# A side chain that waits for its conditioning, weight loads moved from ACT to SP, split sums in the norms, and unused products in a two-block kernel

## The chip, the cores and the metric

The kernel runs on one core of one Trainium2 chip. The metric is the device time of one execution in microseconds (us). Five engines work in parallel, each through its own instructions in the order in which they were written: PE (TensorE, matrix products; its weight loads are listed as PEld), DVE (VectorE), ACT (ScalarE), POOL (GpSimd) and SP (SyncE, which here only issues DMAs). An instruction that waits holds up all that stands behind it on its engine.

## The reference, cut to what matters

Two transformer blocks over 512 tokens of width 1024, all in float32. The first (`first_block`) has a gating unit, a sparse attention, an attention over a memory of 256 tokens, and a feed-forward part. The second (`second_block`) has two layers, and carries a context of 256 tokens beside the 512:

```python
for l in range(DEPTH_2):
    m = (jax.nn.silu(c) @ w_mod[l] + b_mod[l]).reshape(B, N_MOD, D_MODEL)          # conditioning
    mc = (jax.nn.silu(c_ctx) @ w_mod[l] + b_mod[l]).reshape(1, N_MOD, D_MODEL)
    x = ffn_sublayer(x, m, 0, norm_g[l, 0], ffn_w_in[l, 0], ffn_w_out[l, 0])
    xc = ffn_sublayer(xc, mc, 0, norm_g[l, 0], ffn_w_in[l, 0], ffn_w_out[l, 0])   # context
    h, hc = mod_norm(x, m, 1, norm_g[l, 1]), mod_norm(xc, mc, 1, norm_g[l, 1])
    ...                                                 # mixers, attention over h and hc
    x = ffn_sublayer(x, m, 2, norm_g[l, 2], ffn_w_in[l, 1], ffn_w_out[l, 1])
```

`mod_norm` is an RMS norm, scaled and shifted by rows of the conditioning m (or mc). Layer l of the conditioning has nine rows; the second norm (i = 1) reads rows 3 and 4.

## The kernel before

**Products.** A float32 product is made of three passes (lines 388 to 390, or 401 to 406 for a pair of tiles): the weights are split into a high and a low part, `whi` by a copy on ACT (L356) and `wlo` by a subtraction on DVE (L357). Weight tiles `raw` of 512 KB are loaded by SP (L338) in a list of uses. `get` takes the next one, splits two tiles ahead and loads three ahead; there are three buffers for each.

**Conditioning.** `plan` cuts w_mod into 336 parts of 256 KB. One part is a load into one of two buffers `wm` (L576, issued by ACT, one part ahead) and one multiply-and-sum on DVE (L590), or two where x and the context both want it. `get` runs one part (`tick`), unless it is called without. `need_mods` runs on the spot, in a row, all parts that are missing for a row of the conditioning: whoever calls `mods` gets them at that place of DVE's order.

**The side chain.** The context's work is written as a generator, `ctx_chain`, that stands in a queue. `fill(ns)` writes out pieces of it, so many ns worth, between pieces of the main work, mainly in stages in which PE would wait: the sparse attention (`nsa`), `mem_attention` (FILL_MEM, 3650 ns a unit), the norms (`norm_now`), the mixers. A piece that yields a negative cost stops the fill. In its order the chain makes: norm and feed-forward part of the context (`norm_c(0, 0)`, `ffn2`), then `norm_c(0, 1)`, then keys and values (`kv_c`, eight tiles of 24 products of 256 columns), then it waits for the mixers of x. So `norm_c(0, 1)` and `kv_c` are written out in `mem_attention`, before the first block's feed-forward part (`ffn1`, 64 tiles).

**Norms.** The squares of the eight tiles of x are made on ACT and added up, on POOL for the first four and on DVE for the others (`sq_add`); the last is not added but kept as `tail`. `col_rstd` sums over the 128 partitions by products with a column of ones (L478, two for each of the four blocks of 128 tokens), then takes the power on POOL (L429), and `spread` (L487) turns it into a tile.

**Compression.** `compress` in the sparse attention reads eight tiles `fc` of 512 KB, each loaded by SP where it is used (L912, products L915), with two buffers.

## Time and profile before

| | us |
|---|---|
| median of 3 runs (lowest, highest) | 3607.94 (3606.37, 3608.75) |
| the profiled execution | 3608.67 |
| its span, first to last instruction | 3606.9 |
| PE busy in it | 3363.2 |
| DVE busy | 2045.1 |
| ACT busy | 1212.0 |

The profile is one execution. Its time and its span differ by 1.8 us, which lies around the instructions. Of the span PE is idle for 244 us (3606.9 - 3363.2). "PEclk" is the share of the full TensorE clock that was granted in a stretch: 1.00 is 2.4 GHz, 0.50 is 1.2 GHz. Where a row of the order of time ends in [t <-X], the engine was idle for t us before, until X.

### The profile page before, as it was taken

The page shows a single profiled execution, that of the slowest core. Times are in us where ns is not written, and L with a number is a line of the kernel's source. Part 1 is how long each engine was busy: PE and PEld are TensorE (multiplying, and loading weights), DVE is VectorE, ACT ScalarE, POOL GpSimd, SP SyncE. Part 2 cuts the span into 40 slices and gives each one's busy share as a digit, 9 for nine tenths or more (in the row PEclk, how much of TensorE's full clock was granted, in tenths as well). Part 3 has the DMA queues.
Part 4 walks back from the last instruction along what each step waited for, and adds up shares of the span by engine and source line. Part 5 has one row for each costly group of instructions (what it writes and reads, how often), then busy time and mean ns, then how long its engine had stood idle before and what let it go on. Part 6 is the DMA issues. An engine that isn't in the chain of part 4 may idle for free.

```text
span 3606.9 us, 48216 instructions
## 1 busy us (share of the span) xinstructions
PE 3363.2 (93%) x18878; PEld 2935.1 (81%) x18878; DVE 2045.1 (57%) x4231; ACT 1212.0 (34%) x2417; POOL 103.3 (3%) x156
## 2 busy tenths in 40 slices
PE   8969995089999999999999999999999999999999
PEld 7969985068887888788888888888888888878887
DVE  6578665657777766666564444463333454554445
ACT  6335542053333322236542221232122224633222
POOL 1100000010000000000000000010000010000000
PEclk9989997589999999999999999999999999999999
DMA  5444344425443544444333233212212113323332
GB/s 200 168 140 139 119 133 125 136 83 151 147 146 114 154 144 144 130 138 135 107 100 97 91 97 94 74 47 71 65 65 65 60 58 120 99 69 102 98 98 78
DMA packets 143348, 396.79 MB, mean 110 GB/s; under 512 B 16144, under 2 KB 27280, under 8 KB 142608
## 3 DMA queue, kind: packets, MB, share of 16 engines
q1 hardware_dynamic: 94736, 305.61, 26.7%
q10 hardware_dynamic: 48384, 88.10, 8.4%
q8 instruction: 148, 2.42, 0.3%
q14 instruction: 80, 0.66, 0.1%
HBM read 387.36 MB, written 2.10 MB: 108 GB/s over the span
## 4 chain that ended last, share of the span: by engine, by line
PE 83%; DVE 7%; DMA 4%; issue 3%; ACT 3%; POOL 1%; SPq 0%; ACTq 0%; DVEq 0%; POOLq 0%
PE mm L388 19%; PE mm L389 19%; PE mm L390 19%; PE aux L388 5%; PE aux L389 5%; PE aux L390 5%; DMA wm<-in_wmod 3%; DVE wlo L357 1%; PE aux L1748 1%; DVE wm L590 1%; PE mm L416 1%; PE mm L418 1%; PE mm L417 1%; PE mm L401 1%; PE mm L402 1%
## 5 line engine op out<-in xcount | busy, mean ns | idle before, releaser
L357 DVE TENSOR_TENSOR wlo<-raw,whi 128x512 fp32r<-128x512 f32 (+1 forms) x1060 | 692.7, 696 | 452.9 <-ACT whi L356 445.6
L388 PE MATMUL mm<-h,whi 128*128 128x512 f32 (+1 forms) x2352 | 898.3, 382 | 11.1 <-ACT whi L356 10.8
L356 ACT CAST whi<-raw 128x512 fp32r<-128x512 f32 (+1 forms) x1060 | 599.3, 616 | 906.1 <-issue 634.4
L389 PE MATMUL mm<-h,whi 128*128 128x512 f32 (+1 forms) x2352 | 894.3, 380 | 6.4 <-DVE h L512 5.8
L390 PE MATMUL mm<-h,wlo 128*128 128x512 f32 (+1 forms) x2352 | 891.4, 379 | 0.4 <-DVE wlo L357 0.4
L388 PEld LDWEIGHTS mm<-h,whi 128*128 128x128 f32 x2352 | 446.1, 190 | 93.5 <-ACT whi L356 11.0
L389 PEld LDWEIGHTS mm<-h,whi 128*128 128x128 f32 x2352 | 446.2, 190 | 87.7 <-DVE h L512 7.4
L390 PEld LDWEIGHTS mm<-h,wlo 128*128 128x128 f32 x2352 | 445.8, 190 | 83.8 <-DVE wlo L357 0.8
L388 PE MATMUL aux<-h,whi 128*128 128x256 f32 x1056 | 304.1, 288 | 0.7 <-DVE t L509 0.5
L389 PE MATMUL aux<-h,whi 128*128 128x256 f32 x1056 | 301.6, 286 | 0.5 <-DVE h L512 0.3
L390 PE MATMUL aux<-h,wlo 128*128 128x256 f32 x1056 | 301.3, 285 | 0.0
L388 PE MATMUL mm<-g,whi 128*128 128x512 f32 (+1 forms) x720 | 277.9, 386 | 0.0
L389 PE MATMUL mm<-g,whi 128*128 128x512 f32 (+1 forms) x720 | 277.7, 386 | 0.0
L390 PE MATMUL mm<-g,wlo 128*128 128x512 f32 (+1 forms) x720 | 276.7, 384 | 0.0
L590 DVE CUSTOM_DVE_ANT_0 wm<-wm,silu_c 128x512 f32<-128x512 f32 x336 | 232.0, 691 | 67.2 <-DMA wm<-in_wmod 61.0
L1400 DVE SCALAR_TENSOR_TENSOR x<-mm,gate,x 128x512 f32<-128x512 f32 x160 | 120.0, 750 | 180.4 <-PE mm L390 180.3
L388 PEld LDWEIGHTS aux<-h,whi 128*128 128x128 f32 x1056 | 205.0, 194 | 4.9 <-DVE t L509 0.9
L389 PEld LDWEIGHTS aux<-h,whi 128*128 128x128 f32 x1056 | 204.6, 194 | 4.8 <-DVE h L512 1.3
L390 PEld LDWEIGHTS aux<-h,wlo 128*128 128x128 f32 x1056 | 204.6, 194 | 0.0
L421 ACT CAST g<-t 128x512 fp32r<-128x512 f32 x88 | 54.6, 621 | 397.2 <-DVE t L1446 397.2
L1446 DVE SCALAR_TENSOR_TENSOR t<-t,mm 128x512 f32<-128x512 f32 x88 | 60.5, 688 | 212.8 <-PE mm L390 212.4
L390 PEld LDWEIGHTS mm<-g,wlo 128*128 128x128 f32 x720 | 135.3, 188 | 27.5
(364 smaller groups left out, 4898.0 us busy)
## 6 DMA issues: line engine op xcount, KB each, us to landing
raw<-in_w_a SPq DMA_DIRECT2D x220, 512.0 KB, 3.5
wm<-in_wmod ACTq DMA_DIRECT2D x336, 256.0 KB, 2.7
raw<-in_w_d SPq DMA_DIRECT2D x110, 512.0 KB, 3.5
raw<-in_w_in SPq DMA_DIRECT2D x84, 512.0 KB, 3.6
raw<-in_w_f SPq DMA_DIRECT2D x64, 512.0 KB, 3.5
raw<-in_w_out SPq DMA_DIRECT2D x32, 512.0 KB, 3.6
bias<-in_bias SPq DMA_DIRECT2D x64, 128.0 KB, 2.1
raw<-in_w_kv SPq DMA_DIRECT2D x8, 512.0 KB, 4.2
```

Source lines behind the costliest of these rows:

```text
L356: self.nc.scalar.copy(hi[:, cs], raw[:, cs])
L357: self.nc.vector.tensor_tensor(lo[:, cs], raw[:, cs], hi[:, cs].bitcast(F32), op=OP.subtract)
L388: mmul(o, wh[:, k, cols], h[:, k], start=s, stop=False)
L389: mmul(o, wh[:, k, cols], l[:, k], start=False, stop=False)
L390: mmul(o, wl[:, k, cols], h[:, k], start=False, stop=e)
L401: mmul(o, wh[:, k], h[:, k], start=n == 0, stop=False)
L402: mmul(o, wl[:, k], h[:, k], start=False, stop=False)
L416: mmul(o, h[:, k0 + k], wh[:, k], start=s, stop=False)
L421: self.nc.scalar.copy(hi, src)
L590: nc.vector.tensor_tensor_reduce(o, w, self.sc[:, s, ks], 1.0, 0.0, OP.mult, OP.add, wm[:, half, s, j % 8:j % 8 + 1])
L1400: nc.vector.scalar_tensor_tensor(xs, o, gate[:, m:m + 1], xs, op0=OP.mult, op1=OP.add)
L1446: nc.vector.scalar_tensor_tensor(hid, hid, 0.5, b, op0=OP.mult, op1=OP.mult)
```

## The change

- `ctx_chain` yields a negative cost until rows 3 and 4 of the context's conditioning are made, so `norm_c(0, 1)` is not written out before.
- Parts of the conditioning: `project_uv` has eight more ticks; the last tiles of `ffn1` and of `mix_out` have none.
- `wm` is loaded by SP in place of ACT, and `get` issues it ahead of the next `raw`.
- `compress` loads its first two tiles ahead of `project_vg` and each other one two steps ahead.
- Norms: the last two squares are kept as tails. `col_rstd` sums the running sum and tail 6 first, then tail 7 by itself, with one more small operation on DVE.
- `busy(3)` writes three products of constants, that nobody reads, at three places in `norm_now`, each where the queue is empty; and five products of a constant tile stand at the program's start.

```diff
@@ class Body
+    def busy(self, n):
+        p = self.mm()
+        for _ in range(n):
+            self.nc.tensor.matmul(p[:, :256], self.ident, self.cst[:, :256], start=True, stop=True)
@@ get
         assert self.order[i] == key, (self.order[i], key)
+        if tick:
+            self.load_wm()
         self.ensure(i + ahead)
@@ sq_add
-        if m == 7:
-            ss.tail = t
+        if m > 5:
+            ss.tail.append(t)
         else:
             late.append(add)
@@ col_rstd
-        parts = [ss.sum] + [ss.tail] * (ss.tail is not None)
+        if ss.tail:
+            v = self.small(nb)
+            self.token_sums(p, [ss.sum] + ss.tail[:-1], nb)
+            self.nc.vector.tensor_scalar(v, p[:, :nb], 1.0 / dim, EPS, op0=OP.mult, op1=OP.add)
+            p = self.aux()
+            self.token_sums(p, ss.tail[-1:], nb)
+            self.nc.vector.scalar_tensor_tensor(v, p[:, :nb], 1.0 / dim, v, op0=OP.mult, op1=OP.add)
+            return self.rsqrt(v, nb, slow)
+        self.token_sums(p, [ss.sum], nb)
+        return self.rstd(p[:, :nb], nb, 1.0 / dim, slow)
@@ norm_now
+        if not self.queue:
+            self.busy(3)
         self.fill(FILL_A)
         it = self.norm(*args)
         next(it)
+        if not self.queue:
+            self.busy(3)
         self.fill(FILL_S)
         while not ready():
             self.fill(1000)
-        for _ in it:
+        for n, _ in enumerate(it):
+            if n == 0 and not self.queue:
+                self.busy(3)
             self.fill(FILL_B / 4)
@@ load_wm
-            self.nc.scalar.dma_start(w, self.d["wmod"][l, j, half])
+            self.nc.sync.dma_start(w, self.d["wmod"][l, j, half])
@@ block1
+        mem = base.tile([128, 8, TC], F32, tag="xc", name="mem")
+        idle = mem.rearrange("p k n -> p (k n)")[:, :512]
+        nc.vector.memset(idle, 1.0)
+        p = self.mm()
+        for _ in range(5):
+            nc.tensor.matmul(p, idle[:, :128], idle, start=True, stop=True)
...
+                comp = self.compress(ksp, w2, kc, vc, rows, gg)
+                next(comp)
                 self.project_vg(hh, hl, v2, gates, pair)
-                comp = self.compress(ksp, w2, kc, vc, rows, gg)
...
                     if n > 7:
                         next(ln, None)
+                    if n % 2:
+                        self.tick()
@@ compress
+        def load():
+            if todo:
+                ws.append(self.fc(F32))
+                nc.sync.dma_start(ws[-1], self.d["cw1"][todo.pop(0)])
+        load()
+        load()
+        yield 0
...
-                w1 = self.fc(F32)
-                nc.sync.dma_start(w1, self.d["cw1"][i, q])
+                w1 = ws.pop(0)
...
+                load()
                 yield 1700
@@ ffn1
-                    w = self.get(("f2", g, mp_))
+                    w = self.get(("f2", g, mp_), g < 7 or mp_ < 2)
@@ ctx_chain
         self.ffn_ready = True
+        while self.mods_done[1] < 5:
+            yield -1
         yield from self.norm_c(0, 1)
@@ mix_out
-            self.gemm_fm([(p, mh, ml)], self.get((("o", l), m), s == 0))
+            self.gemm_fm([(p, mh, ml)], self.get((("o", l), m), s == 0 and m < 6))
```

DVE's order in `mem_attention`. Before, the end of the run of parts that `norm_c(0, 1)` asks for (it begins 100 products L590 earlier) and the units of the attention behind it (L1255 to L1262):

```order
L590 ISA wm,modp<-wm,silu_c 128x512
L590 ISA modp 128x1
L597 TENSOR_TENSOR mod<-modp 128x2x8
L598 TENSOR_TENSOR mod<-mod,vecs 128x2x8
L616 SCALAR_TENSOR_TENSOR sm<-mod,vecs 128x8
L1479 COPY kp<-sm 128x8
L1283 TENSOR_TENSOR h<-aux,h 128x512
L1255 TENSOR_REDUCE sm<-mm 128x1
L1257 TENSOR_SCALAR sm<-sm,mr 128x1
```

Now, at the same place (L1456 is the context's last addition to xc, L1325 the old L1283, L1297 the old L1255):

```order
L1456 SCALAR_TENSOR_TENSOR xc<-aux,gate,xc 128x256
L466 TENSOR_TENSOR ss<-ss,t_6411 128x256
L1456 SCALAR_TENSOR_TENSOR xc<-aux,gate,xc 128x256
L1325 TENSOR_TENSOR h<-aux,h 128x512
L1297 TENSOR_REDUCE sm<-mm 128x1
L1299 TENSOR_SCALAR sm<-sm,mr 128x1
L1303 RECIPROCAL sm<-sm 128x1
```

The run of products is gone from this place, and behind it the steps of `norm_c` between the units (L509, L512) and the splits for `kv_c` (L357).

SP's order where `project_vg` begins (`raw` are weight tiles, 560 columns those of `project_vg`; `fc` tiles of `compress`). Before:

```order
L338 DMA raw_517<-in_w1_in 128x560
L338 DMA raw_569<-in_w1_in 128x560
L338 DMA raw_641<-in_w1_in 128x1024
L338 DMA raw_676<-in_w1_in 128x1024
L338 DMA raw_733<-in_w1_kv 128x1024
L338 DMA raw_771<-in_w1_kv 128x1024
L338 DMA raw_821<-in_w1_in 128x1024
L912 DMA fc_867<-in_cw1 128x1024
```

Now:

```order
L344 DMA raw_526<-in_w1_in 128x560
L600 DMA wm_576<-in_wmod 128x512
L344 DMA raw_578<-in_w1_in 128x560
L946 DMA fc_642<-in_cw1 128x1024
L946 DMA fc_644<-in_cw1 128x1024
L600 DMA wm_652<-in_wmod 128x512
L344 DMA raw_654<-in_w1_in 128x1024
L600 DMA wm_687<-in_wmod 128x512
L344 DMA raw_689<-in_w1_in 128x1024
```

The first two tiles of `compress` moved ahead of five weight tiles, and a load of `wm` stands before each `raw`; in `ffn1` wm and raw take turns in the same way.

PE's order in the last `norm_now` (layer 1, before the last feed-forward part), now (L497 the sums over partitions, L505 the spread, L409 and L410 the first products of the next part; before, eight sums L478 and then L487 stood there):

```order
L299 MATMUL mm<-cst 128x256 x3
L497 MATMUL aux<-cst,ss 128x1
L497 MATMUL aux<-cst,t_27508 128x1
...
L497 MATMUL aux<-cst,t_27545 128x1 x4
L299 MATMUL mm<-cst 128x256 x3
L505 MATMUL aux<-cst,sm 128x128 x4
L299 MATMUL mm<-cst 128x256 x3
L409 MATMUL mm<-h,whi 128x512
```

Twelve sums stand in place of eight, and nine unused products around them. In the two norms before layer 1's first feed-forward part and its mixers three unused products stand behind the spread; in the norms of layer 0 there are none.

## Rows read from the trace of the kernel before

**Rows 1.** Waits of PE, whole span: us in total, times, longest us.
```profile
PE mm L1271 <- DVE t L1262: 130.4, 2, 130.1
PE aux L985 <- DVE uv L986: 13.4, 3, 12.4
...
PE aux L487 <- POOL sm L429: 8.8, 5, 3.4
...
PE aux L478 <- DVE ss L458: 7.4, 4, 3.2
PE aux L915 <- DMA fc<-in_cw: 6.2, 2, 4.1
```

**Rows 2.** Busy time by stretch: us, then engines with (x instructions), PEclk, DMA.
```profile
594.98:724.35 129.37, 1.91 (x14) 1.36 (x12) 71.93 (x214) 1.12 (x3) 0.00 (x0) 0.51 0.48 138
724.35:772.23 47.88, 38.27 (x240) 33.57 (x240) 30.58 (x79) 26.16 (x66) 0.90 (x2) 0.86 0.27 88
1537.00:1720.00 183.00, 179.35 (x1160) 162.50 (x1159) 123.95 (x271) 94.58 (x192) 1.32 (x24) 1.00 0.47 140
```

**Rows 3.** Line 590 from 586 to 728 us, and what its engine waited for.
```profile
L590 DVE CUSTOM_DVE_ANT_0 wm<-wm,silu_c x68: 685/692/694, 595.0 to 722.9; 128x512 f32<-128x512 f32 x68
...
  DMA wm<-in_wmod: 55.8, 66
```

**Rows 4.** DVE in order of time behind that run: start us, us.
```profile
724.35 0.68 DVE L1283 TENSOR_TENSOR h<-aux,h 128x512 fp32r<-128x512 f32 x1
...
726.87 0.42 DVE L1255 TENSOR_REDUCE sm<-mm 128x1 f32<-128x256 f32 x1
...
728.78 0.42 DVE L1255 TENSOR_REDUCE sm<-mm 128x1 f32<-128x256 f32 x1
```

**Rows 5.** PE in order of time: products of `kv_c`, the attention's last.
```profile
748.47 0.28 PE L388 MATMUL mm<-h,whi 128*128 128x256 f32 x1
...
753.02 0.28 PE L390 MATMUL mm<-h,wlo 128*128 128x256 f32 x1
...
772.23 1.98 PE L1281 MATMUL aux<-mpt,mv 128*128 128x512 f32 x4 [0.46 <-ACT mpt L1272]
```

**Rows 6.** DVE in order of time: first and last forced product of `norm_c(0, 0)`.
```profile
186.37 0.68 DVE L590 CUSTOM_DVE_ANT_0 wm<-wm,silu_c 128x512 f32<-128x512 f32 x1
...
197.50 0.08 DVE L590 DVE_READ_ACCUMULATOR2_ANT modp<- 128x1 f32 x1
```

**Rows 7.** Busy time by stretch around three waits, columns as in rows 2.
```profile
80.00:95.00 15.00, 10.86 (x63) 10.66 (x61) 7.72 (x18) 8.78 (x18) 1.52 (x3) 0.66 0.53 180
...
186.00:201.00 15.00, 2.56 (x19) 2.12 (x17) 8.40 (x29) 0.00 (x0) 0.00 (x0) 0.70 0.49 142
...
3223.90:3237.60 13.70, 9.31 (x38) 8.01 (x38) 7.52 (x13) 3.90 (x6) 1.02 (x1) 0.63 0.05 20
```

**Rows 8.** The same for two stages that get more, or keep, conditioning parts.
```profile
90.00:180.00 90.00, 85.39 (x687) 84.55 (x687) 46.68 (x122) 33.07 (x75) 10.71 (x16) 0.95 0.49 168
180.00:270.00 90.00, 62.78 (x421) 55.91 (x420) 71.38 (x204) 36.02 (x102) 1.50 (x2) 0.85 0.45 141
```

**Rows 9.** Two norms in order of time: behind `ffn1`, and the last one.
```profile
1152.12 0.69 DVE L590 CUSTOM_DVE_ANT_0 wj<-wm,silu_c 128x512 bf16<-128x512 f32 x1
...
1156.43 0.38 PE L478 MATMUL aux<-cst,ss 128*128 128x1 f32 x2 [3.24 <-DVE ss L458]
...
1158.77 0.16 DVE L446 TENSOR_SCALAR sm<-aux 128x4 f32<-128x4 f32 x1 [2.32 <-PE aux L478]
...
3225.36 0.38 PE L478 MATMUL aux<-cst,ss 128*128 128x1 f32 x2 [1.45 <-DVE ss L458]
...
3228.11 0.16 DVE L446 TENSOR_SCALAR sm<-aux 128x4 f32<-128x4 f32 x1 [2.73 <-PE aux L478]
```

**Rows 10.** DMA issues: kind, count, KB each, median us from issue to landing.
```profile
wm<-in_wmod ACTq DMA_DIRECT2D x336, 256.0 KB, 2.7
...
raw<-in_w_f SPq DMA_DIRECT2D x64, 512.0 KB, 3.5
```

More of the change, by code (lines that the diff above doesn't have):

```diff
@@ L210, in __init__ @@
     def __init__(self, ap):
-        self.sum, self.tail = ap, None
+        self.sum, self.tail = ap, []
 class Order(list):
@@ L474, in col_rstd, with token_sums @@
         p = self.aux()
-        parts = [ss.sum] + [ss.tail] * (ss.tail is not None)
+        if ss.tail:
[8 more added lines that the diff above has]
+        return self.rstd(p[:, :nb], nb, 1.0 / dim, slow)
+    def token_sums(self, p, parts, nb):
         for b in range(nb):
@@ L479, in col_rstd @@
                                       stop=i == len(parts) - 1)
-        return self.rstd(p[:, :nb], nb, 1.0 / dim, slow)
     def spread(self, y, nb, p=None, j0=0, step=1):
@@ L665, in block1 @@
                 self.ensure(0)
-        mem = base.tile([128, 8, TC], F32, tag="xc", name="mem")
         nc.sync.dma_start(mem, d["memT"])
@@ L907, in compress @@
         nc = self.nc
+        todo = [(i, q) for i in range(2) for q in range(4)]
+        ws = []
+        def load():
[5 more added lines that the diff above has]
+        yield 0
         for i in range(2):
```

## The prediction

> **What bounds the kernel now.** I read the waits of PE first, because PE is busy for 3363.2 of the 3606.9 us of the span and no other engine is busy for more than 2045.1. A gain therefore has to come out of the 244 us in which PE is idle, or out of stretches in which it runs at less than the full clock. Summed over its lines, PE's waits show one that stands alone [rows 1]: L1271, the transposes of `mem_attention`, waited 130.1 us once. Behind it come L985 with 12.4 us once, the norms (L478 and L487, 16.2 us in ten waits) and the products of `compress` (L915, 6.2 us in two). Then I looked at each place by stretch and in order of time. In the long one PE has 1.91 us of work in 129.37 us, ACT 1.12, and DVE 71.93 [rows 2]: DVE itself is idle for 57 us of it. Line 590 says why: 68 parts are multiplied there from 595.0 to 722.9 us, and their engine waits for the load of `wm` 66 times, 55.8 us in all [rows 3]. So the stall is not DVE's arithmetic; it is a run of loads with two buffers, 129.37 / 68 = 1.90 us a part, and PE's next product stands behind it.
>
> **The chain held.** The 68 parts are forced because `norm_c(0, 1)` asks for row 4 of the context's conditioning before the parts are due. Held back, the chain writes nothing there, and DVE's order goes from the context's last addition straight to the units of the attention. What is left of them is ten units of two heads. The first softmax step of a head is L1255, and two of them stand 728.78 - 726.87 = 1.91 us apart [rows 4] where DVE has no filler between. Ten units at 1.91 and the last additions of L1283 (0.68 each, some three left to be late) give about 21 to 22 us from 595, so that the last products of the attention, which start at 772.23 [rows 5], start at about 617.5. The gross gain is 772.2 - 617.5 = 154.7 us: the run of 129.4, and 25.3 of the 47.88 us behind it, in which PE was busy for 38.27 at a clock of 0.86 with `kv_c` between the units [rows 2].
>
> `kv_c` is not gone, it moves. Emission puts it into the mixers of layer 0, where PE is busy for 179.35 of 183 us at full clock [rows 2]; it is hidden by nothing there. Its products are 0.28 us each at the half clock, as 748.47 shows it [rows 5]. PE passes 128x256 at the full clock in half of that or less; nearest in size, I take 0.12 us: 8 x 24 x 0.12 = 23.0, and 0.8 for its transposes and its norm's sums. From both sides: 3.65 us of idle PE in that stretch could swallow that much (20), and 0.14 each gives 28. I take 24, and one more microsecond for a next stage that begins at the lower level of the clock, 0.51 having been granted through the stall [rows 2]. Net: -154.7 + 24 + 1 = **-129.7** (-133 to -122). The parts themselves now run in the places of their weight tiles, through `ffn1` and on to layer 0's last part; each takes 0.69 us of DVE (a second product where both want it), and a tile of 24 products of 512 columns, twice the 256 above, lasts 24 x 0.24 = 5.8 us of PE by the same estimate, so I cost them at nothing, and price the failure of that cover below.
>
> **The second forced run.** `norm_c(0, 0)` forces seven parts, 186.37 to 197.58 us [rows 6], and PE has 2.56 us of work in the 15 us around at a clock of 0.70 [rows 7]. The eight ticks added in `project_uv` bring 33 parts before that point where 32 are wanted, so the run disappears. PE's wait of 12.4 [rows 1] ends earlier by the run's 11.2, and some of the low clock behind it goes: -12.5 (-8, if h or the chain is what comes next, to -17). The price is 8 x 0.77 (0.68 and 0.08 [rows 6]) = 6.2 us of DVE in a stage where it is busy for 46.68 of 90 us [rows 8]; PE is busy for 85.39 there, so it could cost all of it where DVE is just late. I take +1 (0 to +6).
>
> **Loads of `compress`.** Two waits, 6.2 us together [rows 1], in a stretch of 15 us in which PE is busy for 10.86 at 0.66 [rows 7]. Loads that stand five weight tiles earlier in SP's order have landed by then. The waits go, and of the 10.86 us at 0.66 some 3 to 5 come back with the clock; -10.5 (-13 to -6, when the five weight tiles behind are later instead).
>
> **Norms.** Behind `ffn1` DVE is in a product of the conditioning until 1152.8, and the power waits for the sums at 1156.43, with v at 1158.77 [rows 9]. With the last ticks of `ffn1` gone and the last square not added on DVE, the sums start some 2.8 us earlier: -2.8. In the others the sums of tail 7 stand behind those of the rest, which start earlier, but each norm has four more sums of 0.19 us (0.38 for two [rows 9]), +0.8 each in three norms where PE has other work: +2.4. In layer 1's first norm two parts now stand ahead of the chain's next steps on DVE, +1.5. The last norm has PE busy for 9.31 of 13.70 us at 0.63 [rows 7]; nine unused products fill waits of 1.45 and 2.73 us [rows 9], and if they keep the clock up, some 2.5 of the lost cycles come back: -2.5 (-5 to 0), and -0.7 since one addition of squares (0.68, as large as L1283's) no longer stands ahead of the sums. The unused products of layer 1's other norms stand behind a spread, and I give them -0.3. Sum: **-2.4** (-9 to +4). The trace of before has no unused product; below nothing they cannot go further than the low clock in that window, 9.31 x 0.37 = 3.4, and above it they cost nine times 0.12 to 0.28.
>
> **SP's loads.** ACT loses 336 issues, but it is busy for a third of the span and ends none of PE's long waits. SP issues in order, and now waits for a free `wm` ahead of a `raw`. A `raw` lands 3.5 us behind its issue, `wm` 2.7 [rows 10]; three tiles of `raw` are on hand, of over 5 us of PE each in the long stages. I take 0 (-4 to +12). By the Trainium skill, page "DMA: Bandwidth & Descriptors", section "Queues, rings and completion order", each pair of a queue row and an engine is a ring of its own, and an engine goes round between the rows that have work. Two issuers then share an engine where one is served in order. By that rule `wm` stands behind the `raw` issued ahead of it; the rows show no such pair on one queue.
>
> **Start.** The five products end before x has landed; -0.5 (-1.8 to +0.5).
>
> The sum: -129.7 - 12.5 + 1 - 10.5 - 2.4 + 0 - 0.5 = -154.6. From the profiled execution, 3608.67 - 154.6 = 3454.1; that execution is 0.7 us above the median (3607.94), which moves nothing. Forecast: **3454 us**, by the terms' bounds (taken together loosely, not all at one end) 3440 to 3468.
>
> **Rivals.** *The forced parts cost elsewhere, in part.* SP's one queue is now in order, and a `wm` may land behind a `raw`: 2.7 + 3.5 = 6.2 us from issue [rows 10], with a `get` each 5 us. It decides in the sparse attention and the context's part, where tiles are short: from 180 to 270 us DVE is busy for 71.38 of 90 [rows 8], so it has 18.6 us to spare. Some 15 parts stand there; 15 x 3.5 = 52 us later, less 18.6, is 34 of stall: 3454 + 34 = 3488. A lighter form is `kv_c` and the parts in the mixers pushing DVE (123.95 of 183 us before [rows 2]) onto PE's path, about +15: 3469. For it: 55.8 us of waits for `wm` where parts run close [rows 3]. Against it: those are runs without tiles between them. The Trainium skill's rule on rings, cited above, would make this case the right one; the same page's section "Issuing engines are not separate DMA queues" has all issuers use the same 16 engines, which speaks for nothing being lost.
>
> *A larger gain.* If the clock stays up in all the norms and the early loads and ACT's relief shorten `compress` and the attention as well, the ends of the terms that are below add up: -17 for -12.5, -13 for -10.5, -9 for -2.4, -4 for 0, -133 for -129.7, together -21: 3433.
>
> *It doesn't do what it says.* The hold ends at `norm_c` asking for rows 3 and 4, but some other call of `mods` could force the same 68 parts a stage later. At 1.90 us a part that is 129: 3454 + 129 = 3583. The order of after shows no run of L590 longer than a few.
>
> *Slower.* SP waits for DVE at each of the 336 loads of `wm`, and each `raw` behind it is that much late. The three tiles on hand cover it until they are used up; past that PE waits at each tile. It decides from 154 / 336 = 0.46 us a load: at 0.6 us a load the loss is 202, and the time 3454 + 202 = 3656. Against it: a part's buffer is free a whole tile before its next load.
>
> **How the numbers follow.** Forecast 0.60; larger gain 0.11; later loads or uncovered work (3468 to 3500) 0.24; not doing what it says 0.02; slower 0.03. The range goes from 3436 to 3482: it leaves out some 0.07 below and some 0.12 above. Faster by over 0.2% (7 us, about what a measurement of this kernel can tell from no change) 0.96, within it 0.01, slower 0.03.
>
> **What will show it.** In the waits of PE, L1271's successor without its 130 us, L985's without its 12.4, L915's without its 6.2. Line 590 without the run from 595, and its parts spread to layer 0's last part. Products of `kv_c` between the mixers' tiles, at 0.12 us each, 23 in all. SP: the landing of `raw` not above 3.5, DVE's waits for `wm` far below the 55.8 us of the run of before [rows 3]; if they stand at `get` in the attention, the first rival is right. The clock of the last norm above 0.63. The prediction is wrong if the attention over the memory still ends much behind 620 us, if the mixers of layer 0 lengthen by over 30, or if `ffn1` is longer than before.

## The result and the profile after

The changed kernel takes 3466.82 us in the median of four runs (3462.17 to 3473.68), the kernel before 3608.35 beside it. The ratio is 0.961, 95% interval 0.9592 to 0.9628: 3.9% faster, 141.5 us less. The prediction was 3454 us with a range of 3436 to 3482, so the time lies in the range, 12.8 us above the forecast. The profiled execution took 3464.53 us with a span of 3462.8; of that execution the shortfall is 3464.5 - 3454.1 = 10.4 us, and it is the one that is taken apart here.

The waits of PE in the changed kernel, whole span (engine, tile and line <- who was waited for: us in total, times, longest us). L1313 is the line that was L1271 before:

```profile
PE mm L1313 <- DVE t L1304: 12.0, 8, 2.8
PE aux L505 <- POOL sm L437: 7.6, 3, 4.6
...
PE aux L973 <- ACT tc L964: 2.1, 1, 2.1
```

The wait of 130.1 us [rows 1] is gone, and eight small ones of at most 2.8 us stand on that line. The wait of 12.4 us has left one of 0.7, and the 6.2 us for `fc` of rows 1 have no successor. The line that multiplies the parts, L614 now, over the whole span:

```profile
L614 DVE CUSTOM_DVE_ANT_0 wm<-wm,silu_c x336: 676/691/1108, 39.4 to 2766.6; 128x512 f32<-128x512 f32 x168
...
  DMA wm<-in_wmod: 6.6, 9
```

DVE waited for `wm` 66 times in the forced run alone, 55.8 us [rows 3]; now it is 9 times and 6.6 us in the whole program. Three stretches of the changed kernel, in the columns of rows 2 (us; PE, PEld, DVE, ACT, POOL; PEclk): around the loads of `compress`, the units of the memory attention, and the last norm.

```profile
80.00:95.00 15.00, 14.93 (x129) 14.73 (x128) 8.46 (x20) 11.14 (x25) 1.72 (x3) 1.00 0.56 186
573.00:598.00 25.00, 14.42 (x45) 7.88 (x46) 11.46 (x40) 10.23 (x33) 0.00 (x0) 0.83 0.00 0
...
3080.00:3094.00 14.00, 13.70 (x77) 11.48 (x76) 6.52 (x14) 3.32 (x5) 1.02 (x1) 1.00 0.11 37
```

The clock at 80 us was 0.66 before and is 1.00; in the last norm it was 0.63 and is 1.00 [rows 7].

To see where the time went I cut both traces at the same products and compared the lengths. "Clock lost" is half of PE's busy time in stretches that were granted 1.2 GHz; "work" is what is left of a stage without idle time and lost clock. All are us, before / after, and the forecast is what the terms of the prediction say for that stage.

| stage | length | change | forecast | idle PE | clock lost | work |
|---|---|---|---|---|---|---|
| start to the end of `compress` | 149.8 / 137.7 | -12.1 | -10.0 | 17.6 / 5.4 | 7.4 / 1.7 | 124.8 / 130.6 |
| into the sparse attention, to the seventh group of its output products | 103.1 / 91.4 | -11.7 | -12.5 | 27.5 / 13.9 | 6.0 / 9.2 | 69.6 / 68.4 |
| to the last transposes of the memory attention | 518.5 / 367.0 | -151.5 | -154.7 | 146.0 / 21.8 | 11.4 / 8.1 | 361.1 / 337.1 |
| to `ffn1` | 24.5 / 25.9 | +1.4 | +1 | 0.5 / 0.5 | 0.0 / 1.5 | 24.0 / 23.9 |
| `ffn1` and the norm behind it | 367.9 / 365.0 | -2.9 | -2.8 | 9.8 / 7.7 | 4.4 / 2.7 | 353.7 / 354.6 |
| layer 0's first feed-forward part and a norm | 370.0 / 369.6 | -0.4 | 0 | 4.7 / 2.2 | 3.2 / 3.1 | 362.2 / 364.4 |
| mixers of layer 0, to their last transposes | 214.2 / 242.0 | +27.8 | +24 | 4.6 / 5.3 | 1.5 / 5.4 | 208.1 / 231.3 |
| to layer 1's first feed-forward part | 676.3 / 682.6 | +6.3 | +3.1 | 10.8 / 9.9 | 5.1 / 10.1 | 660.4 / 662.6 |
| layer 1 to its attention | 672.4 / 674.3 | +1.9 | +0.5 | 4.4 / 3.1 | 1.7 / 2.4 | 666.3 / 668.9 |
| to the last feed-forward part, and it | 510.2 / 507.3 | -2.9 | -3.2 | 18.0 / 13.3 | 5.9 / 1.7 | 486.3 / 492.3 |

Idle PE fell by 161 us in all. The clock that is lost did not fall: 46.6 us in these stages before, 45.9 after. It left the places at which the prediction looked (`compress`, the last norm) and stands at others. The work grew by 18. `kv_c` is not in that: it left the attention (24.0 less) and came to the mixers (23.2 more). What grew is the stages with unused products and more sums, the first and the last above all. In the first, the products at the start only stand where PE was idle: without them ("No unused products" below) its work is 124.8 and its idle time 11.8.

### The profile page after: what moved, and what is told of

Same layout as the page of the kernel before. It is cut to its first block, busy times and chain, and to the rows that moved or that the text cites. A ratio compares the mean times of both kernels' runs of the same rounds, so it can differ in the third digit from the quotient of the medians.

```text
span 3462.8 us, 48551 instructions
## 1 busy us (share of the span) xinstructions
PE 3379.8 (98%) x18978; PEld 2946.4 (85%) x18978; DVE 2036.4 (59%) x4232; ACT 1211.0 (35%) x2417; POOL 105.3 (3%) x156
## 4 chain that ended last, share of the span: by engine, by line
PE 86%; DVE 7%; ACT 3%; issue 2%; DMA 1%; POOL 0%; SPq 0%; ACTq 0%; DVEq 0%; POOLq 0%
PE mm L396 20%; PE mm L397 20%; PE mm L398 20%; PE aux L396 5%; PE aux L397 5%; PE aux L398 5%; DVE wlo L363 2%; PE aux L1792 1%; PE mm L424 1%; PE mm L426 1%; PE mm L425 1%; PE mm L409 1%; PE mm L410 1%; PE mm L414 1%; PE aux L1178 1%
## 5 line engine op out<-in xcount | busy, mean ns | idle before, releaser
L614 DVE CUSTOM_DVE_ANT_0 wm<-wm,silu_c 128x512 f32<-128x512 f32 x336 | 231.6, 691 | 12.9 <-DMA wm<-in_wmod 6.6
```

Of the source, the lines that this page charges most:

```text
L614: nc.vector.tensor_tensor_reduce(o, w, self.sc[:, s, ks], 1.0, 0.0, OP.mult, OP.add, wm[:, half, s, j % 8:j % 8 + 1])
```

## The experiments

The changed kernel ran again beside three of its variants.

### The changed kernel again

No edit.

> The changed kernel as it is, beside the three below on one chip. Both theories: 3462 to 3474 us. If the 8 us that the mixers of layer 0 lost to a low clock are a matter of the single execution (theory A), this profile has stretches at half clock there of another length; if they belong to the order of the work (theory B), two stretches of some 10 and 7 us stand again right behind the attention over the context, with PE busy through them.

3466.03 us (3463.88 to 3473.66), ratio 0.9612 (0.9599 to 0.9625). The mixers' stage, the columns as above:

```profile
1361.30:1602.80 241.50, 236.13 (x1596) 217.91 (x1597) 164.84 (x355) 129.16 (x266) 1.32 (x24) 0.98 0.42 136
```

It is 241.5 long with 4.7 us of clock lost, as in the first execution (242.0 and 5.4). So within one order of the work this loss came back at about its size, as theory B said. But the lost clock of all stages is 51.6 here where it was 45.9, and the places in which it differs are others: the stage of the two attentions lost 14.2 in place of 8.1, that of `compress` 0.0 in place of 1.7. This execution is 9 us longer than the first (span 3471.9), and idle PE accounts for 2 of them. A spread of this size is the grain of every comparison below.

### The kernel before, looked at again

No edit.

> The kernel before, looked at once more for its clock. Theory A (where PE loses clock differs between executions of one kernel, and its total is about the same in both kernels): 45 to 60 us lost in all, with several stages 3 us or more away from the first profile. Theory B (the changed order loses clock that the kernel before did not lose in the mixers): the mixers of layer 0 up to their last transposes lose 1.5 us again, and the later stages up to layer 1 5 us.

One execution, 3611.01 us. The same stage of its mixers, to be held against 214.2 us at 0.99 in the first execution:

```profile
1533.20:1750.50 217.30, 212.67 (x1401) 194.44 (x1401) 145.07 (x315) 114.38 (x234) 1.32 (x24) 0.98 0.44 132
```

Here the kernel before lost 4.8 us of clock in the mixers, not 1.5, so against this execution the mixers of the changed kernel are 24.7 us longer: the forecast's 24. So what the mixers took beyond the forecast is no more than what two executions of the kernel before differ by. In the stage behind it, which runs to layer 1, the kernel before lost 4.2 us again (5.1 at first), and the changed kernel 10.1 and 10.6: there theory B holds, and in these four executions some 5 us go with the changed order.

### The hold alone

```diff
         self.ffn_ready = True
+        while self.mods_done[1] < 5:
+            yield -1
         yield from self.norm_c(0, 1)
```

> The kernel before with one edit: the side chain yields until rows 3 and 4 of the context's conditioning are made. Prediction: -129.7 by itself, so 3478 us (3475 to 3486), with the run of 100 products gone and 24 us more in the mixers of layer 0. Rival (the hold only pays together with the loads by SP or the added parts): the wait comes back at a later place, and the time is over 3500.

3492.33 us (3490.35 to 3495.79) against 3609.93, ratio 0.9679 (0.9664 to 0.9693): -117.6, where -129.7 was forecast for this edit, and above the 3475 to 3486 that were expected. The waits of PE in it:

```profile
PE aux L985 <- DVE uv L986: 12.2, 1, 12.2
PE mm L388 <- ACT whi L356: 11.5, 2, 8.2
PE mm L1271 <- DVE t L1262: 11.3, 8, 3.2
```

The long wait is gone by this edit alone, and the wait of 12.4 of rows 1 stays, as it must. Up to the attention's last transposes the stage went from 518.5 to 367.6, -150.9 (forecast -154.7). To `ffn1` it is +2.8 (forecast +1), all of it lost clock, and the mixers are +29.1 (forecast +24): 23.1 of work, as forecast, 1.1 of idle time and 4.9 of clock. In the stage behind them it is +3.5 with the same work, 2.2 of it clock and 1.2 idle time. So the move of `kv_c` cost what it was said to cost, the attention is 3.8 us longer than said, and most of the rest is clock.

### The change without the hold

```diff
         self.ffn_ready = True
-        while self.mods_done[1] < 5:
-            yield -1
         yield from self.norm_c(0, 1)
```

> The changed kernel without the hold. Prediction: the forced run of parts is back in mem_attention, somewhat shorter by the eight parts that are made earlier (8 x 1.90 = 15), and the time is 130 - 15 = 115 us above the changed kernel, near 3582. Rival (loads by SP, which stand ahead of each raw, shorten the forced run too): less than 100 above.

3583.35 us (3581.58 to 3584.41), ratio 0.9929 (0.9915 to 0.9944), 117.3 above the changed kernel: 115 was expected. The run is back. Line 614 from 560 to 720 us:

```profile
L614 DVE CUSTOM_DVE_ANT_0 wm<-wm,silu_c x68: 681/692/694, 568.4 to 694.4; 128x512 f32<-128x512 f32 x68
...
  DMA wm<-in_wmod: 54.1, 61
```

My reason for 115 was wrong all the same. I said that eight parts fewer would be forced; 68 stand there again, since the eight early ones had only taken the place of the seven that `norm_c(0, 0)` forced before. From its first product to its last it takes 126.0 us (568.4 to 694.4), where it took 127.9 (595.0 to 722.9 [rows 3]). The hold is worth some 117 here as in the kernel before.

### The loads of wm by ACT again

```diff
-        if tick:
-            self.load_wm()
         self.ensure(i + ahead)
...
-            self.nc.sync.dma_start(w, self.d["wmod"][l, j, half])
+            self.nc.scalar.dma_start(w, self.d["wmod"][l, j, half])
```

> The changed kernel with the loads of wm issued by ACT again, and not ahead of raw. Theory of the prediction (SP's order costs nothing): the same as the changed kernel within 5 us, waits of DVE for wm a few us in either. Rival (one ring served in order delays wm and raw): 10 to 34 us faster than the changed kernel, and fewer waits for raw and wm.

3477.84 us (3475.77 to 3479.7), ratio 0.9641 (0.9627 to 0.9654): 11.8 us slower than the changed kernel, and the two intervals don't meet. Neither theory had this sign. ACT in order of time, where `project_uv` and `compress` alternate (a row of ACTq is the DMAs that ACT issues; with x2 it runs from the start of the first issue to the end of the second):

```profile
107.94 5.33 ACTq L598 DMA_DIRECT2D wm<-in_wmod  x2
113.32 0.47 ACT L932 ACTIVATE uv<-mm,pair 128x256 f32<-128x256 f32 x1 [6.46 <-DVE mod L619]
116.26 0.31 ACT L962 ACTIVATE tc<-aux,sm 128x62 f32<-128x62 f32 x1 [2.47 <-DVE sm L961]
...
136.89 3.10 ACTq L598 DMA_DIRECT2D wm<-in_wmod  x2
140.04 0.48 ACT L932 ACTIVATE uv<-mm,pair 128x256 f32<-128x256 f32 x1 [3.44 <-DVE modp L612]
```

A load of `wm` is written when its buffer is not yet free. On ACT the second of the two loads in the 5.33 us waits there for DVE's product, and the activation behind it (L932), which has nothing to do with conditioning, starts at 113.32, some 3.5 us after PE's last product for it. But nothing on PE waited for that activation. PE's waits from 75 to 165 us in this kernel:

```profile
PE aux L971 <- ACT tc L962: 6.8, 1, 6.8
PE aux L991 <- DVE vc L994: 1.0, 1, 1.0
```

The 6.8 us end with the activation L962 at 116.26, which itself waited for DVE (L961), and on DVE parts of the conditioning stood ahead of L961 and waited for their loads:

```profile
112.20 0.69 DVE L612 CUSTOM_DVE_ANT_0 wm<-wm,silu_c 128x512 f32<-128x512 f32 x1 [3.09 <-DMA wm<-in_wmod]
...
115.46 0.69 DVE L612 CUSTOM_DVE_ANT_0 wm<-wm,silu_c 128x512 f32<-128x512 f32 x1 [2.15 <-DMA wm<-in_wmod]
...
116.08 0.22 DVE L961 TENSOR_TENSOR sm<-aux,vecs 128x1 f32<-128x1 f32 x2
```

ACT had issued these two loads at 105.29 and 107.94, and they landed 6.8 and 7.5 us later. SP meanwhile had issued two larger loads, the context (1 MB, at 105.58) and a tile `fc` (512 KB, at 106.48), and the DMA engines were busy for 0.96 of the time from 105 to 110 us. In the changed kernel SP waits for the buffers of `wm` ahead of these two loads, issues them at 109.27 and 110.21, and three loads of `wm` before them land 2.6, 2.6 and 3.2 us behind their issue. So by these rows the gain at this place is the order of the loads on one queue, `wm` before larger ones, and not ACT's time. In the whole program DVE waits 18.7 us for `wm` here, in twelve waits, and 6.6 in the changed kernel. An order like that with ACT as issuer was not tried.

In the changed kernel the same wait (L973, the first fence) is 2.1. In the kernel before, where ACT loaded `wm` too but eight parts fewer stood in `project_uv`, it was 1.5 (0.4 with the hold alone):

```profile
PE aux L931 <- ACT tc L922: 1.5, 1, 1.5
```

At the end of `compress` this kernel stands 6.5 us behind the changed one (144.2), and at the sparse attention's output products 9 to 10. SP has the same wait for the buffer, but only loads stand behind it, `raw` with tiles on hand.

### Tiles of compress loaded where they are used

```diff
-        load()
-        load()
         yield 0
...
+                load()
                 w1 = ws.pop(0)
...
-                load()
                 yield 1700
```

> The changed kernel with each of compress's tiles loaded where it is used, as before. Prediction: the two waits of 4.1 and 2.1 us and the low clock around them are back, +10.5 (6 to 13). Rival (only the waits count, the clock recovers anyway): +6 or less.

3492.74 us (3488.12 to 3498.44), ratio 0.968 (0.9664 to 0.9697): 26 to 27 us slower than the changed kernel's two medians (3466.8 and 3466.0), two and a half times the forecast 10.5. PE's waits from 75 to 165 us, and then SP's from 70 to 165 us, where L946 is the load of `fc`, L600 that of `wm` and L344 that of `raw`:

```profile
PE aux L955 <- DMA fc<-in_cw: 17.1, 3, 8.7
```

```profile
SPq L600 <- DVE modp L614: 25.9, 14, 5.1
SPq L344 <- DVE wlo L363: 23.1, 2, 14.7
```

So the waits for these tiles are not the 6.2 us of rows 1 but 17.1, with 9.9 us of clock lost beside them (7.4 before).

### The same with wm by ACT

The two diffs above together.

> The changed kernel with compress's tiles loaded where they are used and wm by ACT, so as both were before. Theory A (late tiles of compress are dear only because wm by SP stands ahead of them): it is faster than late tiles with wm by SP (3493), near 3478 + 10 = 3488, and PE waits some 6 us for these tiles in place of 17. Rival (late tiles cost 26 us whatever the queue): 3478 + 26 = 3504.

3489.01 us (3483.29 to 3494.73), ratio 0.9664 (0.9642 to 0.9686). PE's waits from 75 to 165 us:

```profile
PE aux L953 <- DMA fc<-in_cw: 6.4, 2, 3.6
PE aux L969 <- ACT tc L960: 5.5, 1, 5.5
```

Theory A gave 3488, the rival 3504. With `wm` on ACT the tiles are late by 6.4 us, as in rows 1, and the early loads are worth 3489.0 - 3477.8 = 11.2, near the forecast's 10.5. With `wm` on SP they are worth 26, because a late load of `fc` then stands behind SP's waits for DVE. The two edits cover each other: had these loads not been moved ahead, moving `wm` to SP would have gained nothing that these runs show. The medians of the two kernels with late tiles differ by 3.7 us, which their intervals don't tell apart; the waits do.

The kernel of this run has the eight added parts in `project_uv`, with `wm` on ACT and the tiles of `compress` late as before. It reaches the end of `compress` at 154.9 us; the kernel before, in its two executions, and the kernel with the hold alone reach it at 149.8, 152.1 and 150.0. DVE waits 15.8 us for `wm` from 75 to 165 us here, and 9.4 in the kernel before. So beside loads by ACT the added parts seem to cost 3 to 5 us there, and part of what SP's loads gave in the changed kernel is that this cost stays away. SP's loads without the added parts were not tried.

### The eight parts of project_uv

```diff
                     if n > 7:
                         next(ln, None)
-                    if n % 2:
-                        self.tick()
```

> The changed kernel without the eight added parts in project_uv. Prediction: norm_c(0, 0) forces seven parts again, PE waits some 12 us there, and 1 us of DVE's work ahead comes back: +11.5 (7 to 16). Rival (the wait is then hidden, since loads of wm come earlier by SP): within 4.

3472.75 us (3469.31 to 3479.67), ratio 0.9626 (0.9611 to 0.964): 6.7 us slower by the medians, and the intervals overlap. The trace is clearer. PE's longest wait from 165 to 215 us is back in full:

```profile
PE aux L1025 <- DVE uv L1026: 13.2, 3, 12.2
PE mm L1114 <- ACT t L1106: 2.2, 1, 2.2
```

The stage is 99.2 long in place of 91.4 and 90.3: 8 to 9 us. The stage before it, with `compress`, is 1.1 shorter (136.6 in place of 137.7 and 137.8), which is the price of DVE's work as forecast. The forecast 11.5 took the whole wait as the gain. In the changed kernel PE has other waits at this place; those of 2.4 and 1.2 us stand in the kernel without the parts too (2.2 and 1.2), the one of 3.3 and most of the 1.3 don't:

```profile
PE mm L505 <- DVE cs L1084: 3.3, 1, 3.3
PE mm L1116 <- ACT t L1108: 2.4, 1, 2.4
PE aux L1178 <- DVE t L1162: 1.3, 1, 1.3
PE mm L505 <- DVE mk L1256: 1.2, 1, 1.2
```

### No unused products

```diff
-        if not self.queue:
-            self.busy(3)
         self.fill(FILL_A)
...
-        nc.vector.memset(idle, 1.0)
-        p = self.mm()
-        for _ in range(5):
-            nc.tensor.matmul(p, idle[:, :128], idle, start=True, stop=True)
```

(The other two places of `norm_now` likewise.)

> The changed kernel without the unused products, those at the start among them, and without the fill of the tile that these read. Prediction: 2.8 us slower in the norms (the last norm again at a mean clock near 0.63) and 0.5 at the start, together +3 (0 to +7). Rival (the unused products only lengthen the norms): up to 3 us faster, with the clock of the last norm unchanged.

3471.98 us (3466.43 to 3476.01), ratio 0.9624 (0.961 to 0.9637): 6 us slower by the medians, with intervals that overlap. In the trace two things are plain. The last norm is at 0.67 again where the changed kernel has 1.00:

```profile
3089.50:3103.20 13.70, 10.76 (x51) 9.19 (x50) 6.67 (x13) 3.52 (x5) 1.02 (x1) 0.67 0.12 39
```

From layer 1's attention to the end this kernel is 2.7 us longer than the changed one (136.3 + 373.7 against 136.0 + 371.3), and the forecast for the products there was 2.5. In layer 1's two other norms, where three of them stand behind the spread, the work of the two stages is 1.4 and 1.3 us less without them than in the changed kernel beside it; but their idle time is 1.2 and 1.3 more, and the stages are as long (685.2 and 676.6 us without them, 685.3 and 676.5 with). PE in order of time in the changed kernel's last norm (three products are six entries):

```profile
3082.54 1.46 PE L299 MATMUL mm<-cst 128*128 128x256 f32 x6
...
3086.43 1.54 PE L299 MATMUL mm<-cst 128*128 128x256 f32 x6
```

They are 0.49 us each and not the 0.12 to 0.28 that I took from `kv_c`'s products of the same 256 columns. At the start the first product of `compress` stands at 79.3 us without them and at 79.2 and 80.2 with them: no gain there, where 0.5 was forecast. The whole stage to the end of `compress` is 2.1 us longer without them (139.9 in place of 137.7 and 137.8), most of it in clock lost later in the stage (3.3 in place of 1.7 and 0.0); one execution doesn't show whether that comes of the start.

### The norms' sums as before

```diff
-        if m > 5:
+        if m > 6:
             ss.tail.append(t)
...
-        if ss.tail:
-            v = self.small(nb)
...
-            return self.rsqrt(v, nb, slow)
-        self.token_sums(p, [ss.sum], nb)
+        self.token_sums(p, [ss.sum] + ss.tail, nb)
         return self.rstd(p[:, :nb], nb, 1.0 / dim, slow)
```

> The changed kernel with one square kept as tail and the sums of all in one piece, as before; the unused products and the left out parts of the conditioning stay. Prediction: the split gives 0.7 in the last norm and 1 to 2 behind the first feed-forward part, and costs 2.4 in three others, so within 2 us of the changed kernel. Rival (the split is what makes the norms short): 2 us slower in each of five norms, +10.

3464.98 us (3461.38 to 3467.33), ratio 0.9605 (0.9592 to 0.9618): 1 us faster, not to be told from the changed kernel. Behind `ffn1` the split is worth about 1 us (365.9 in place of 365.0 and 364.8), from layer 0's first part to its mixers another 0.8, in the last stage 1.0 (508.3 in place of 507.3), and it costs about as much where PE has other work. The split sums pay for nothing in all.

### A version that beats both: the attention's units in two steps

With the chain held, nothing fills the time between a unit's steps. DVE in the changed kernel ran the row maximum of a unit (L1297) at 575.6, 577.4, 581.8 and 583.8: a unit takes 1.9 us, and the last one of a head 4.4, since the head's two output products, their copy on ACT (L1324) and DVE's addition behind it (L1325) stand ahead of the next maximum:

```profile
575.59 0.42 DVE L1297 TENSOR_REDUCE sm<-mm 128x1 f32<-128x256 f32 x1
...
577.44 0.42 DVE L1297 TENSOR_REDUCE sm<-mm 128x1 f32<-128x256 f32 x1
...
581.23 0.69 DVE L1325 TENSOR_TENSOR h<-aux,h 128x512 fp32r<-128x512 f32 x1 [1.85 <-ACT h L1324]
581.84 0.41 DVE L1297 TENSOR_REDUCE sm<-mm 128x1 f32<-128x256 f32 x1
```

The edit writes a unit's product, maximum and exponential (`a`) ahead of the reciprocal and scaling of the unit before (`a2`), and all of it ahead of the output products (`cc`).

```diff
+                P[un] = pr, s
+
+            def a2(un):
+                pr, s = P[un]
                 nc.vector.reciprocal(s[:, 1:2], s[:, :1])
                 nc.vector.tensor_scalar(pr, pr, s[:, 1:2], None, op0=OP.mult)
                 P[un] = pr
...
-            for c in self.pipeline([(h, b) for h in range(4) for b in range(4)], a, bb, cc):
+            units = [(h, b) for h in range(4) for b in range(4)]
+            for i in range(len(units) + 3):
+                for lag, f in ((0, a), (1, a2), (2, bb), (3, cc)):
+                    if 0 <= i - lag < len(units):
+                        f(units[i - lag])
+                self.step()
                 self.fill(FILL_MEM)
```

> The changed kernel with one step of mem_attention's units moved: a unit's product and row maximum are written ahead of the reciprocal and scaling of the unit before, and ahead of the head's output products. Now that the chain has nothing to write there, a unit takes 1.9 us by the round trip from DVE to ACT and back, and a head's last one 4.4. Theory A (that stretch is bound by this round trip): ten units at some 1.2 us and no more 2.5 us at two heads' ends, 10 to 13 us less in the attention, 3453 to 3456 in all. Rival (PE's half clock or the copies on ACT bound it): within 3 us of the changed kernel.

3459.27 us (3455.33 to 3460.71), ratio 0.9582 (0.9567 to 0.9597): 7 us less than the changed kernel by the medians, each beside its own kernel before, with an interval of the ratio that lies below (0.9599 to 0.9625). DVE in order of time, the row maxima of four units that now follow each other:

```profile
569.37 0.41 DVE L1297 TENSOR_REDUCE sm<-mm 128x1 f32<-128x256 f32 x1
...
570.40 0.42 DVE L1297 TENSOR_REDUCE sm<-mm 128x1 f32<-128x256 f32 x1
...
571.52 0.42 DVE L1297 TENSOR_REDUCE sm<-mm 128x1 f32<-128x256 f32 x1
...
572.56 0.42 DVE L1297 TENSOR_REDUCE sm<-mm 128x1 f32<-128x256 f32 x1
...
576.44 0.41 DVE L1297 TENSOR_REDUCE sm<-mm 128x1 f32<-128x256 f32 x1
```

A unit takes 1.0 to 1.1 us; the step to a next head still takes 3.9, for the addition of that head waits for ACT's copy of the output products and stands ahead of the next maximum. Of the forecast 10 to 13 us the stage gave 9.6 and 14.3 (357.4 against 367.0 and 371.7). Of the 9.6, 4.8 is idle PE and 6.4 lost clock that came back, with 1.6 more work. So the round trip bound this stretch, but more than half of the gain came with the clock, which the theory had not counted. Its clock was 0.99, against 0.83 in the changed kernel:

```profile
562.00:588.00 26.00, 19.25 (x86) 11.50 (x85) 16.21 (x56) 14.50 (x43) 1.86 (x3) 0.99 0.04 16
```

### The same with the norms' sums as before

Both diffs together.

> The same with the norms' sums of before (one tail, one piece), which were no slower alone. Theory: 1 us less than with the split sums, which is below what can be told; rival (the split pays): 2 us or more above.

3455.4 us (3454.11 to 3459.62), ratio 0.9575 (0.956 to 0.959). It is 3.9 us below the one with the split sums, which the intervals don't tell apart, and 11 below the changed kernel, which they do. This is the fastest version here.

## Why the prediction was right, and where it missed

**The chain held.** The mechanism is the one that was told: the forced run is gone by that one edit, it is back without it, and `kv_c` costs 23 us of PE in the mixers. The net was 117 us both ways, not 129.7, which is outside the term's own bounds (-133 to -122). Two parts of it were mis-sized. "Ten units at 1.91 us" left out that a head's last unit takes 4.4: some 3 to 4 us (the stage gave -150.9 and -151.5 for -154.7). And the one microsecond for the clock behind the move was too little. In the kernel with the hold alone the stretch to `ffn1` lost 2.9 and the mixers 6.4; there the kernel before lost nothing in the one, and 1.5 in one execution and 4.8 in another in the other. Two small readings were off and carry nothing: rows 1 has nine waits of L478 and L487, not ten, and "21 to 22 us from 595" ends at 616 to 617, not at 617.5.

**The second forced run.** The run went, and the stage gave -11.7 for -12.5. But two edits made that: the eight parts 8 to 9 us, SP's loads some 3. The step that failed is that the whole wait was taken as the gain; other waits, the longest of 3.3 us, took part of its place. The price on DVE was right, +1.1 for +1.

**Loads of compress.** -12.1 in the stage for -10.0, and again two edits in one: the early loads of `fc`, and `wm` on SP. Undone with `wm` on SP they cost 26 us, with `wm` on ACT 11.2. Within this stage the early loads gave 10.7 (144.2 in place of 154.9) and SP's loads 6.5 (137.7 in place of 144.2), more together than the 12.1, since the stage with both undone is longer than in the kernel before.

**SP's loads.** This term was forecast at 0, and it is the step that failed outright: undone in the changed kernel it is worth -11.8, well below its own bounds of -4 to +12. I had looked at whether ACT's issues cost time, and at the median landing of `wm` (2.7 us), and not at when it lands beside SP's larger loads. What the runs showed in its place is 6.8 and 7.5 us for two loads issued by ACT in `project_uv`, with DVE and then ACT and PE waiting for them, and 2.6 to 3.2 in SP's order. The rows were there to be asked for: in the trace of before, DVE waited for `wm` from 36 to 190 us as well, outside the long run:

```profile
DVE wm L590 <- DMA wm<-in_wmod: 14.1, 9, 4.3
```

Activations of L902 stood behind loads there too (5.4 us in two, 2.2 in one), as the one of L932 did with `wm` on ACT again.

The total did not come out lower for it, since most of what it gave stood already, under other names, in the two terms above. In the kernel before PE waited only 1.5 us for this ACT (L931), so some of the 11.8 is what the eight added parts would have cost on ACT, and no run shows SP's loads alone in the kernel before. That the total came within 13 us of the forecast is in part luck: with `wm` left on ACT it would have been 3477.8, near the upper end of the range, and what brought it down from there was forecast at nothing.

The Trainium skill's rule on rings (page "DMA: Bandwidth & Descriptors", section "Queues, rings and completion order"), by which `wm` would stand behind `raw` on one queue, gave the first rival its ground. `wm` landed 2.7 us behind its issue, as in rows 10, and a `raw` of the feed-forward part 3.7 where it took 3.5 and should not have taken more:

```profile
wm<-in_wmod SPq DMA_DIRECT2D x336, 256.0 KB, 2.7
...
raw<-in_w_f SPq DMA_DIRECT2D x64, 512.0 KB, 3.7
```

So of the rival's later loads, 3.5 us each, 0.2 came. What one queue cost was shown by the late tiles of `compress` alone, and there SP waited for DVE before the issue.

**Norms.** The sum was -2.4; by the stages from `ffn1` on, less the mixers, it was +2.0. Behind `ffn1` (-2.9 for -2.8) and in the last norm (2.7 for 2.5) the steps were right. An unused product costs 0.49 us and not 0.12, but in layer 1's two other norms that lengthened nothing, since it stands in PE's idle time. The miss is the stage up to layer 1, where 5 us of clock were lost and 3.1 of the 6.3 had been forecast.

**The stage up to layer 1.** The 5 us stand in part in one place, behind the mixers, where PE is busy with narrow work: sums of one column, transposes, products of 64 columns. In the changed kernel PE was granted half the clock for 10.2 us there without being idle. The same 21 us of the changed kernel and, after it, of the one with the hold alone:

```profile
1655.00:1676.00 21.00, 20.82 (x110) 18.85 (x109) 8.28 (x20) 7.40 (x18) 1.02 (x1) 0.76 0.08 26
```

```profile
1685.00:1706.00 21.00, 20.62 (x120) 18.47 (x120) 11.46 (x27) 7.82 (x19) 1.02 (x1) 0.84 0.15 42
```

The kernel before is at 0.92 there, with 78 products of 256 columns and more among the narrow ones in its 21 us; the changed kernel has 36, and the one with the hold alone 55. But a slower stretch also holds fewer products for being slower. The move of `kv_c` is not the cause: the kernel without the hold, whose mixers hold no `kv_c`, is at 0.76 there too, with 39 wide ones. Nor is it any other edit that was undone: the kernels with `wm` on ACT, without the parts in `project_uv`, without the unused products, with the norms' sums as before and with the late tiles lose 9.7 to 10.7 us in this stage, as the changed kernel does (10.1 and 10.6; before 5.1 and 4.2, and 7.3 with the hold alone). Of the change no run undid the parts that are left out of the last tiles of `ffn1` and of `mix_out`. What the cause is stays open.

**The rivals.** The larger gain did not come: the clock came back where it was looked for, and went elsewhere. Nor did a forced run at another place, nor waits of PE for `raw`. The lighter form of the first rival gave 3469, nearer to 3466.8 than the forecast, but its mechanism did not come: in the mixers PE's idle time went from 4.6 to 5.3 us. Nor did the slower one: SP did wait for DVE ahead of its loads (in the changed kernel as in that with late tiles 25.9 us before `wm` from 70 to 165 us), but PE's waits for split weights (`whi` and `wlo`) fell from 15.4 us in all to 7.3. Of the signs that would have made the prediction wrong none came: the attention's last transposes begin at 596.1 us, the mixers are 27.8 longer, and `ffn1` is 2.9 shorter.

## What to carry to other kernels

Which queue a load is issued from also sets which loads go before it. On SP the wait for a free buffer of `wm` kept larger loads back, which cost nothing where tiles were on hand and let `wm` land in 2.6 to 3.2 us in place of 6.8 and 7.5; ahead of a late `fc` it cost 17.1 us of waits. Follow a wait to its last link before naming its cause: PE waited for ACT, that activation for DVE, and DVE for a load. When a stall is removed, go through the rows of the stage once without it. Here the round trips and waits that it had covered were the next bound, and they could be shortened. Where two edits touch one queue, price each with the other done and undone: the early loads were worth 11 us or 26.

## What the hardware showed that I had not expected

Clock was lost in all kernels, 38 to 60 us a span, and removing waits did not reliably bring it down: 46.6 and 49.4 in two executions of the kernel before, 45.9 and 51.6 of the changed one, 37.8 and 38.5 of the two fastest. PE was granted half the clock in a stretch in which it was busy throughout, and had been for 20 us before: the 10.2 us in the place above. And a product of 128x256 by a constant took 0.49 us at the full clock, where one of the same columns in `kv_c` took 0.12, as these rows of the changed kernel in order of time show:

```profile
1381.15 0.29 PE L426 MATMUL mm<-whi,h 128*128 128x256 f32 x1
1381.27 0.28 PE L424 MATMUL mm<-whi,h 128*128 128x256 f32 x1
1381.39 0.28 PE L425 MATMUL mm<-wlo,h 128*128 128x256 f32 x1
```

They start 0.12 us apart; `mm<-cst` took 1.46 for three. In the code the operands of `kv_c` are held as fp32r, those of the unused products as plain float32; that this is the reason was not tried.
